# A third chunk of the contraction formed with Strassen's seven products in nine pairs of column blocks

## The chip, the cores and the metric

The kernel runs on one core of a Trainium2 chip. The metric is device time in microseconds (us) of one execution. TensorE multiplies, VectorE and ScalarE do elementwise work, GpSimd very little, and SyncE issues nearly all transfers.

## The reference

One layer of a hybrid encoder on x of shape (256, 2048) in float32. The part that matters here is a row of dense products, all with 2048 as the contracted length:

```python
h = rms_norm(x, norm_g)
proj = h @ w_in            # q, k, v, o, z, gates, xb, zb, ga, gb
ya = mlstm_branch(...)     # (256, 2048)
yb = rglru_branch(...)     # (256, 2048)
ya = ya @ w_branch_a
yb = yb @ w_branch_b
merged = sigmoid(ga) * ya + sigmoid(gb) * yb
y = rms_norm(x + merged @ w_out, final_g)
```

## The kernel before

**Precision.** TensorE multiplies in a reduced float32 format. Every operand is kept as a high part and a low part (x = hi + lo), and a product is the sum of three matmuls: hi by hi, hi by lo, lo by hi. So every weight tile that is loaded has to be split: ScalarE copies it into `whi` (line 124 or 160), VectorE subtracts it to make `wlo` (line 125 or 161).

**Tiling.** A weight matrix is cut into column blocks of 512 and into eight chunks of the contraction, each of 2 x 128 rows (`KC = 2`). One chunk of one block is a tile of 128 x 1024 (512 KB), loaded by SyncE into one of five `raw` buffers and split into one of four `whi` and one of four `wlo` buffers. The left operand has 256 rows, two blocks of 128. A chunk of one block takes 2 x 2 x 3 = 12 matmuls of 512 columns.

**The nine pairs.** In the last 40% of the kernel, column blocks are computed two at a time by `pair` (lines 144 to 231): two pairs each of w_branch_b (wb), the gb and the ga columns of w_in, and w_branch_a (wa), and one of w_out (wo). Between the wa pairs and the wo pair, one more block of wo is computed in plain form (`block_nat`). In a pair, the chunks listed in `S_WB`, `S_GB`, `S_GA`, `S_WA` and `S_WO` (lines 27 and 28) are not multiplied plainly. Such a chunk is seen as a 2 x 2 block matrix (two blocks of rows by two k halves, times two k halves by two column blocks), and Strassen's method in Winograd's form gives its four results with seven products instead of eight, each of three matmuls:

```python
t1[:, lf] = r1[:, rt_] - r1[:, lf]      # VectorE, 128x512 each
t1[:, rt_] = r2[:, lf] - r1[:, rt_]
t2[:, lf] = t1[:, rt_] + r1[:, lf]
t2[:, rt_] = r2[:, rt_] - t2[:, lf]
mm(p1, *xb(0, 0), b[:, lf], b[:, rt_], last)
mm(p5, *sf(0), h1[:, lf], l1[:, lf], last)
mm(p7, *sf(2), h1[:, rt_], l1[:, rt_], last)
mm(p6, *sf(1), h2[:, lf], l2[:, lf], last)
```

The remaining three products are added straight to the accumulators of the plain chunks. `b` is a split of half a tile (128 x 512, hi and lo side by side), and h1, h2, h3 with l1, l2, l3 are three `whi` and `wlo` tiles made from t1, t2 and the second loaded tile r2. The products p1, p5, p6 and p7 are gathered over the product chunks in four banks of the accumulator memory and combined once after the last of them by one ScalarE copy and four VectorE additions (lines 220 to 224). The chunks up to the last product chunk are run for both blocks in turn, the ones after it for one block and then for the other; at the end of each block comes an addition of the accumulator (line 230) and an epilogue. The plain chunks of a pair go through `load_chunk`.

**Forms.** The left operands of four of the seven products are sums of blocks of the left matrix. `make_form` (lines 233 to 247) makes them once for each chunk and each left matrix (yb, h, ya and m): an addition of hi and lo (line 239; not for yb), four 128 x 128 operations (lines 242 to 245), a ScalarE cast (246) and a VectorE low part (247). The result lies in one of four slots of the slot `PT` (for m in `E`). Its scratch has the tag `vhi`, of which there is one buffer; t1 of every product chunk has the same tag, and t2 has `vlo`. The forms of h are used by the gb and the ga pairs.

**Order.** The program is written in order, and a planner sets the final order on each engine from priorities and from its own model of time. The loads, splits and combinations stand in `urgent()` blocks, the forms don't.

Of the kernel before, what the change touches and what calls it, by code (L numbers as in the profile page):

```python
# [23 lines left out]
EPS = 1e-6  # L24
NEG = -1e30

S_WB, S_GB, S_GA, S_WA = [((0, 4), (0, 4))] * 4
S_WO = (0, 4)

PK_NORM, PK_HEAD, PK_CB, PK_CW, PK_BRG, PK_LAM = 0, 1, 2, 3, 7, 11  # L30
BLK_Q, BLK_K, BLK_V, BLK_O, BLK_Z, BLK_XB, BLK_ZB, BLK_GA, BLK_GB = 0, 2, 4, 8, 12, 16, 20, 24, 28
# [7 lines left out]
def hybrid_encoder(ctx: ExitStack, tc: tile.TileContext, x, xt, pk, bif, fg, wg, wi, wr, wa, wb, wo, out):  # L39
# [19 lines left out]
    def sl(tag, dt=F32, cols=4096):  # L59
        return slot.tile([P, cols], dt, tag=tag, name=name("s" + tag))  # L60
# [172 lines left out]
    def make_form(fm, full=None, parts=None):  # L233
        u = hp.tile([P, 2 * NB], F32, tag="vhi", name=name("sf"))
        if full is None:
            full = u[:, NB:]
            hi, lo = parts
            v = full if len(hi.shape) == 2 else full.rearrange("p (k s) -> p k s", s=S)
            dve.tensor_add(v, f(hi), f(lo))
        a11, a21, a12, a22 = [full[:, i * P:(i + 1) * P] for i in range(4)]  # L240
        s1, s2, s3, s4 = [u[:, i * P:(i + 1) * P] for i in range(4)]
        dve.tensor_add(s1, a21, a22)
        dve.tensor_sub(s2, s1, a11)
        dve.tensor_sub(s3, a11, a21)
        dve.tensor_sub(s4, a12, s2)
        act.copy(fm[:, :NB], u[:, :NB])
        dve.tensor_sub(fm[:, NB:], u[:, :NB], f(fm[:, :NB]))
# [674 lines left out]
    et_ = sl("E", F32R)  # L922
    mf_ = {kq: et_[:, i * 1024:(i + 1) * 1024] for i, kq in enumerate(S_WO)}
    for kq in S_WO:
        make_form(mf_[kq], parts=[t(kq * NB, (kq + 1) * NB) for t in (mh, ml)])
# [5 lines left out]

    pair((wo[0], wo[1]), mh, ml, mf_, S_WO, dst, b11, epi_wo)

# [91 lines left out]
```

## Time and profile before

| | |
|---|---|
| runs (three), median | 1030.87 us (1030.67 to 1031.13) |
| profiled execution | 1030.37 us, span from first to last instruction 1028.6 us |
| TensorE matmuls | 1019.5 us busy, 5124 of them |
| VectorE | 786.2 us busy, 1039 instructions |
| ScalarE | 580.1 us busy, 763 instructions |
| transfers | 199.32 MB, mean 194 GB/s |

Busy time is a union over an engine's instructions, so that overlapping ones are counted once. Matmuls are pipelined: the recorded length of one overlaps the next, and what one costs is read from the distance between starts. The stretch from 594 to 998.5 us holds the nine pairs.

### The profile page before, as it was taken

To read this page: it belongs to the slowest core of one execution; us is meant where nothing else is said; L and a number is where in the kernel's file an instruction comes from. 1 tells how busy PE (TensorE), PEld (TensorE's weight loads), DVE (VectorE), ACT (ScalarE), POOL (GpSimd) and SP (SyncE) were. 2 spreads that over 40 slices of the span, in tenths; PEclk is the share of its full clock that TensorE was granted. 3 is DMA by queue.
4 is the path that set the end of the run, shared out by engine and by line. 5 is a ranking of instruction groups with operands and counts; after the bars stand their busy time and mean duration, and the time that the engine had idled before them with its cause. 6 is when DMAs were issued, how large, how long until landed. Compare 5 with 4: busy or idle time off the path is not lost.

```text
span 1028.6 us, 13664 instructions
## 1 busy us (share of the span) xinstructions
PE 1019.5 (99%) x5124; PEld 867.3 (84%) x5124; DVE 786.2 (76%) x1039; ACT 580.1 (56%) x763; POOL 11.3 (1%) x35
## 2 busy tenths in 40 slices
PE   9999999999999999999999999999999999999997
PEld 9988888888888888888888888888888888888886
DVE  6787797596578649854977778887787877979784
ACT  7545457745765585559455555545554555454562
POOL 1000000000000000000000000000000000000000
PEclk9999999999999999999999999999999999999999
DMA  9654445554555555554655455555566645666562
GB/s 349 255 188 140 164 162 177 175 203 167 182 201 187 183 179 180 191 190 156 212 184 187 163 203 197 211 209 183 194 204 208 214 167 206 212 244 255 183 205 82
DMA packets 55954, 199.32 MB, mean 194 GB/s; under 512 B 6352, under 2 KB 6864, under 8 KB 55504
## 3 DMA queue, kind: packets, MB, share of 16 engines
q1 hardware_dynamic: 55024, 197.13, 55.1%
q10 hardware_dynamic: 864, 1.32, 0.4%
q8 instruction: 40, 0.66, 0.3%
q14 instruction: 26, 0.21, 0.1%
HBM read 196.33 MB, written 2.10 MB: 193 GB/s over the span
## 4 chain that ended last, share of the span: by engine, by line
PE 98%; DMA 1%; DVE 0%; SPq 0%; ACT 0%; issue 0%; DVEq 0%
PE acc L275 16%; PE acc L157 11%; PE acc L154 11%; PE acc L156 11%; PE acc L139 9%; PE acc L140 9%; PE acc L141 9%; PE acc L278 8%; PE aux L154 2%; PE aux L157 2%; PE aux L156 2%; PE aux L761 1%; PE aux L675 1%; PE aux L674 1%; PE aux L673 1%; PE aux L951 1%
## 5 line engine op out<-in xcount | busy, mean ns | idle before, releaser
L125 DVE TENSOR_TENSOR wlo<-raw,whi 128x1024 fp32r<-128x1024 f32 (+1 forms) x321 | 389.3, 1219 | 154.6 <-ACT whi L124 152.6
L124 ACT CAST whi<-raw 128x1024 fp32r<-128x1024 f32 (+1 forms) x321 | 334.4, 1048 | 267.7 <-PE acc L141 80.9
L275 PE MATMUL acc<-sHL,whi 128*128 128x512 f32 x704 | 178.6, 394 | 0.0
L139 PE MATMUL acc<-whi,sHL 128*128 128x512 f32 x416 | 162.4, 390 | 0.0
L140 PE MATMUL acc<-wlo,sHL 128*128 128x512 f32 x416 | 162.2, 390 | 0.0
L141 PE MATMUL acc<-whi,sHL 128*128 128x512 f32 x416 | 162.0, 389 | 0.0
L275 PEld LDWEIGHTS acc<-sHL,whi 128*128 128x128 f32 x704 | 127.0, 189 | 23.7
L278 PEld LDWEIGHTS acc<-sHL,wlo 128*128 128x128 f32 x704 | 96.1, 190 | 7.2
L156 PE MATMUL acc<-wlo,sHL 128*128 128x512 f32 x260 | 101.1, 389 | 0.0
L157 PE MATMUL acc<-whi,sHL 128*128 128x512 f32 x260 | 101.1, 389 | 0.0
L154 PE MATMUL acc<-whi,sHL 128*128 128x512 f32 x260 | 99.5, 389 | 0.0
L278 PE MATMUL acc<-sHL,wlo 128*128 128x256 f32 x704 | 99.2, 283 | 0.0
L141 PEld LDWEIGHTS acc<-whi,sHL 128*128 128x128 f32 x416 | 78.1, 188 | 16.3
L139 PEld LDWEIGHTS acc<-whi,sHL 128*128 128x128 f32 x416 | 78.2, 188 | 15.6
L140 PEld LDWEIGHTS acc<-wlo,sHL 128*128 128x128 f32 x416 | 78.2, 188 | 15.3
L160 ACT CAST whi<-t 128x1024 fp32r<-128x1024 f32 x36 | 37.9, 1053 | 57.4 <-PE acc L157 41.2
L157 PEld LDWEIGHTS acc<-whi,sHL 128*128 128x128 f32 x260 | 48.8, 188 | 10.2
L156 PEld LDWEIGHTS acc<-wlo,sHL 128*128 128x128 f32 x260 | 48.8, 188 | 10.2
L154 PEld LDWEIGHTS acc<-whi,sHL 128*128 128x128 f32 x260 | 48.8, 188 | 10.1
L161 DVE TENSOR_TENSOR wlo<-t,whi 128x1024 fp32r<-128x1024 f32 x36 | 44.0, 1223 | 14.6 <-ACT whi L160 14.6
L156 PE MATMUL acc<-wlo,sA 128*128 128x512 f32 x104 | 40.6, 390 | 0.0
L157 PE MATMUL acc<-whi,sB 128*128 128x512 f32 x104 | 40.5, 390 | 0.0
(314 smaller groups left out, 1435.2 us busy)
## 6 DMA issues: line engine op xcount, KB each, us to landing
raw<-wi SPq DMA_DIRECT2D x255, 512.0 KB, 3.6
raw<-wb SPq DMA_DIRECT2D x32, 512.0 KB, 3.7
raw<-wa SPq DMA_DIRECT2D x32, 512.0 KB, 3.7
raw<-wo SPq DMA_DIRECT2D x32, 512.0 KB, 4.4
raw<-wr SPq DMA_DIRECT2D x8, 512.0 KB, 3.6
sB<-x SPq DMA_DIRECT2D x4, 512.0 KB, 8.3
sA<-x SPq DMA_DIRECT2D x1, 2048.0 KB, 7.4
sA<-xt SPq DMA_DIRECT2D x7, 256.0 KB, 7.2
```

What stands on the lines that cost most here:

```text
L124: last_copy[0] = act.copy(hi[:, r], raw[:, r]).ins
L125: last_sub[0] = dve.tensor_sub(lo[:, r], raw[:, r], f(hi[:, r])).ins
L139: pe.matmul(ps[tb], a, wh, start=(k == 0), stop=False)
L140: pe.matmul(ps[tb], a, wl, start=False, stop=False)
L141: pe.matmul(ps[tb], b, wh, start=False, stop=(k == KT - 1))
L154: pe.matmul(ps, a, wh, start=id(ps) not in began, stop=False)
L156: pe.matmul(ps, a, wl, start=False, stop=False)
L157: pe.matmul(ps, b, wh, start=False, stop=stop)
L160: act.copy(hi, v)
L161: dve.tensor_sub(lo, v, f(hi))
L275: pe.matmul(ps[m], hi[:, o:o + P], hl_t[:, 2 * k * S:2 * (k + 1) * S], start=(k == 0), stop=False, skip_group_check=True)
L278: pe.matmul(ps[m][:, :S], lo[:, o:o + P], hhi(k * S, (k + 1) * S), start=False, stop=(k == KT - 1), skip_group_check=True)
```

## The change

The product form is used for the chunks 0, 2 and 4 of each pair in place of 0 and 4. Chunk 2 was a plain chunk for both blocks. For each of the nine pairs that means seven products where there were eight, one more b, t1, t2 and three more splits of 128 x 1024 in place of two; and one more form for each of yb, h, ya and m. The last product chunk is still 4, so that the combination stays where it was. The host lays out the weights of chunk 2 as those of 0 and 4. The slots that forms are put in follow from the order in the lists: for yb 0, 1 and 2 in place of 0 and 1; for h slot 3, and then 0 and 1 in place of 0; for ya slot 2, and then 0 and 1 in place of 0.

```diff
-S_WB, S_GB, S_GA, S_WA = [((0, 4), (0, 4))] * 4
-S_WO = (0, 4)
+S_WB, S_GB, S_GA, S_WA = [((0, 2, 4), (0, 2, 4))] * 4
+S_WO = (0, 2, 4)
```

## Rows read from the trace of the kernel before

**Rows 1.** The page: busy time, the chain that ended last, a group of casts.
```profile
PE 1019.5 (99%) x5124; PEld 867.3 (84%) x5124; DVE 786.2 (76%) x1039; ACT 580.1 (56%) x763; POOL 11.3 (1%) x35
...
PE 98%; DMA 1%; DVE 0%; SPq 0%; ACT 0%; issue 0%; DVEq 0%
...
L160 ACT CAST whi<-t 128x1024 fp32r<-128x1024 f32 x36 | 37.9, 1053 | 57.4 <-PE acc L157 41.2
```

**Rows 2.** Windows (busy by engine, clock, DMA): wb pair 2, gb pair 1, wo, all.
```profile
636.50:678.50 42.00, 42.00 (x187) 34.79 (x186) 36.41 (x46) 21.46 (x23) 0.00 (x0) 1.00 0.58 201
678.50:720.50 42.00, 42.00 (x188) 34.75 (x186) 33.44 (x35) 21.57 (x22) 0.00 (x0) 1.00 0.57 200
...
931.50:956.00 24.50, 24.50 (x118) 20.36 (x117) 21.95 (x28) 12.29 (x16) 0.00 (x0) 1.00 0.67 257
...
sum 404.50, PE 404.50 PEld 334.99 DVE 335.38 ACT 213.45 POOL 0.00; mean PE 40.45 PEld 33.50 DVE 33.54 ACT 21.35 POOL 0.00
```

**Rows 3.** Timeline of TensorE (start, length): first and last of 30 matmuls.
```profile
695.79 0.39 PE L154 MATMUL acc<-whi,sHL 128*128 128x512 f32 x1
...
702.37 0.39 PE L157 MATMUL acc<-whi,sHL 128*128 128x512 f32 x1
```

**Rows 4.** Timeline of VectorE, gb pair 2, from pair end to pair end.
```profile
720.70 1.22 DVE L230 TENSOR_TENSOR sD<-sD,acc 128x1024 f32<-128x1024 f32 x1 [0.37 <-PE acc L157]
...
729.48 1.22 DVE L125 TENSOR_TENSOR wlo<-raw,whi 128x1024 fp32r<-128x1024 f32 x1
730.61 0.69 DVE L161 TENSOR_TENSOR b<-raw,b 128x512 fp32r<-128x512 f32 x1
731.21 0.69 DVE L176 TENSOR_TENSOR t<-raw,raw 128x512 f32<-128x512 f32 x1
731.93 0.69 DVE L180 TENSOR_TENSOR t<-t,raw 128x512 f32<-128x512 f32 x1
...
762.86 1.22 DVE L230 TENSOR_TENSOR sD<-sD,acc 128x1024 f32<-128x1024 f32 x1 [0.36 <-PE acc L157]
```

**Rows 5.** Waits of VectorE and of ScalarE, 594 to 1000 us (total, times, longest).
```profile
DVE wlo L161 <- ACT whi L160: 31.4, 30, 1.5
...
ACT whi L124 <- PE acc L157: 62.0, 64, 1.7
ACT whi L160 <- PE acc L157: 61.6, 41, 1.9
...
ACT whi L160 <- DVE t L181: 8.3, 4, 3.1
```

**Rows 6.** Timeline ahead of gb: two forms, t1, low part, TensorE's first use.
```profile
652.60 0.69 DVE L239 TENSOR_TENSOR sf<-sHL 128x512 f32<-128x512 f32 x1
653.32 0.29 DVE L242 TENSOR_TENSOR sf<-sf 128x128 f32<-128x128 f32 x1
...
656.78 0.68 DVE L247 TENSOR_TENSOR sPT<-sf,sPT 128x512 fp32r<-128x512 f32 x1
...
666.23 0.69 DVE L247 TENSOR_TENSOR sPT<-sf,sPT 128x512 fp32r<-128x512 f32 x1
...
668.57 0.69 DVE L175 TENSOR_TENSOR t<-raw 128x512 f32<-128x512 f32 x1
...
672.64 1.22 DVE L161 TENSOR_TENSOR wlo<-t,whi 128x1024 fp32r<-128x1024 f32 x1
...
679.02 0.39 PE L156 MATMUL aux<-wlo,sPT 128*128 128x512 f32 x1
```

**Rows 7.** Timeline ahead of wo: second form, low part, TensorE's first use.
```profile
941.88 0.68 DVE L239 TENSOR_TENSOR sf<-sHL 128x512 f32<-128x512 f32 x1
...
946.60 0.68 DVE L247 TENSOR_TENSOR sE<-sf,sE 128x512 fp32r<-128x512 f32 x1
...
951.00 1.22 DVE L161 TENSOR_TENSOR wlo<-t,whi 128x1024 fp32r<-128x1024 f32 x1
...
957.53 0.39 PE L156 MATMUL aux<-wlo,sE 128*128 128x512 f32 x1
```

## The prediction

> **What bounds the kernel now.** I read the page first: TensorE's matmuls are busy 1019.5 us of a 1028.6 us span, and the chain of work that ended last is 98% TensorE [rows 1]. Next I cut the time in which the nine pairs run (594 to 998.5 us) into ten windows, one for each pair and one for the plain block ahead of the last pair [rows 2]. TensorE is busy in all 404.50 us of them at a granted clock of 1.00, which is the 2.4 GHz level; VectorE is busy 335.38 us (83%), ScalarE 213.45 us (53%), and the DMA engines about 0.6 of the time. So a matmul left out here shortens the kernel by one step of the matmul stream, as long as the weight tiles keep coming. The timeline of TensorE gives that step [rows 3]: 29 matmuls of 512 columns lie between the starts 695.79 and 702.37 us, so 6.58 / 29 = 0.2269 us each (a matmul's recorded 0.39 us overlaps the next). Two ends of a pair, 720.70 and 762.86 us [rows 4], are 42.16 us apart for 186 matmuls: the same 0.2267 us.
>
> The reader should then look at VectorE, since it is the engine that the change loads. In the list of waits [rows 5], ScalarE's copies of weight tiles waited 62.0 us (plain tiles) and 61.6 us (product tiles) for TensorE to finish with an old tile, and only 8.3 us for VectorE. That is back-pressure: four buffers each of whi and wlo are full and the preparation is ahead. VectorE's own wait for the copies of product tiles, 31.4 us, is mostly the same back-pressure handed on.
>
> **What the change does, part by part.**
>
> *Matmuls.* A chunk of a pair takes 2 x 2 x 2 x 3 = 24 matmuls in plain form and 7 x 3 = 21 in product form. Nine pairs give 27 matmuls fewer, each with its weight load, which runs beside the matmuls: 27 x 0.2267 = 6.12 us. All of it lies on the path that sets the end.
>
> *VectorE, chunks.* Two plain subtractions go and eight operations come: one 512-wide for b, four 512-wide for t1 and t2, three 1024-wide for the low parts. By recorded length [rows 4] that is 5 x 0.69 + 3 x 1.22 = 7.1 against 2 x 1.22 = 2.4. But consecutive operations overlap: in the same rows a 1024-wide one that starts at 729.48 is followed at 730.61 (step 1.13 us), and 512-wide ones step by 0.60 (730.61 to 731.21) or, where one reads what the last wrote, 0.72 (731.21 to 731.93). By steps it is about 3.1 + 3.4 = 6.5 against 2.27, so 4.2 us more for each of nine chunks, 37.8 us.
>
> *VectorE, forms.* Four forms are added. One for the wb pairs lies before 594 us, where this window's sum doesn't count it. The ones of h, ya and m lie inside: the add steps 0.72 (652.60 to 653.32 [rows 6]), four 128-wide operations of 0.29 us recorded step about 0.2 each, the low part 0.60, together 1.95 us; three make 5.9 us.
>
> *The balance.* VectorE goes from 335.4 to 335.4 + 37.8 + 5.9 = 379.1 us, and the time it has shrinks from 404.5 to 398.4: 95%, with 19.3 us left. By pair: the first gb pair goes to 33.44 + 4.2 = 37.6 of 41.3 us, which is easy; the second wb pair to 36.41 + 4.2 + 1.95 = 42.6 of 41.3, over by 1.3 us, which the first gb pair can take; the plain wo block to 21.95 + 1.95 = 23.9 of 24.5 [rows 2]. Within a pair the new order is product, plain, product, plain, product: one product and one plain chunk cost VectorE 6.5 + 2.3 = 8.8 us while TensorE takes (21 + 24) x 0.2267 = 10.2 us, so the lead holds. A plain tile feeds 12 matmuls (2.7 us), and a copy and a subtraction after a buffer comes free take about 2.4 us, so the buffers carry a local shortage of two to five us.
>
> The Trainium skill, page "VectorE: DVE Perf Modes", section "The DRAIN you can't avoid", says that a next operation does not start until the pipe has emptied, and so speaks against the change. Here the rows show the next one starting 0.09 us before the recorded end of the one in front (730.61 against 729.48 + 1.22 = 730.70). By the rule the time would be that of rival D below, by the rows it is the sum above.
>
> *ScalarE.* Four casts replace two: three of 1.05 us [rows 1] and one half as wide (0.6 us by that) instead of two of 1.05 us, 1.7 us for a chunk, 15 us in all, and four small casts. 213 becomes about 231 of 398 us; other work doesn't queue up behind it.
>
> *DMA.* A product chunk loads the same two 512 KB pieces as two plain chunks do, on the same queue in the same order: nothing, and the cover is not thin, as the share is about 0.6. The extra instructions are small.
>
> *The one order that tightens.* t1 and every form use one buffer (tag vhi). So all forms made between two pairs must end before the next pair's t1 may start, and behind that t1 stand the cast of h1, the low part and TensorE's first product. Before gb this chain holds two forms: the first runs from 652.60 to the end of its low part at 657.46, the second from there to 666.92, t1 starts at 668.57, the low part of h1 runs from 672.64 to 673.86, and TensorE wants it at 679.02 [rows 6]: 5.2 us of margin. A third form costs between 1.95 us (nothing but its work) and 9.5 us (what the second took, with recombination and plain tiles in between); nearest is the first one's 4.9 us, which fits. The extreme would stall TensorE by 9.5 - 5.2 = 4.3 us. Before wo the chain holds two forms and gets a third: the second takes 941.88 to 947.2, the low part of h1 starts at 951.00 and ends at 952.2, and TensorE wants it at 957.53 [rows 7], so 5.3 us of margin against 1.95 to 5.4 us. Before wa a second form is added too, but by the code the old one is written into a slot that the last product chunk still reads and has to wait for it, so the new one, whose slot is read by the middle chunk, fits into that wait. I take 0.5 us of stall in all; the bounds are 0 and about 5.
>
> *Sum.* The profiled execution took 1030.37 us, 1.77 more than its span; the runs' median is 1030.87. 1030.37 - 6.12 + 0.5 = 1024.75 for that execution, so 1025.25 against the median: 1025.2.
>
> **The rivals.**
> A, the forecast: TensorE stays fed but for small gaps, 1024.3 to 1026.3. For it: TensorE without a gap, and the copies' 123 us of waits for full buffers. Chance 0.60.
>
> B: VectorE sets the pace at a few places, above all at the entries of gb and wo and where two wa pairs meet (there each block has two more 1024-wide operations). It loses 1.5 to 5 us of the 6.1: 1026.4 to 1029.9. For it: the second wb pair's sum over 41.3 us. Against: free VectorE time in the next pair. Chance 0.20.
>
> C, the other side: product chunks bring handshake waits that don't go away. A product tile waits in turn for VectorE's t, ScalarE's cast, VectorE's low part; VectorE waited 31.4 us before such low parts in 18 chunks, 1.74 us each. If those stayed and nine chunks added theirs, the stage would take 379.1 + 27 x 1.74 = 426 us, 21.6 us longer: about 1052. It decides from the point where more than 404.5 - 379.1 = 25.4 us of VectorE's waits can't be filled; just beyond it the time is 1033 to 1036. Against: ScalarE's own waits say that these are full buffers, 61.6 us for TensorE against 8.3 us for t. Chance 0.11, mostly near the point.
>
> D: VectorE is held for each operation's recorded length. 1.22 us in place of a step of 1.13 is 8% more, so the 379.1 us become 409.4, which is 4.9 us longer than the stage is now: 1035.8. The steps in [rows 4] are against it. Chance 0.03. This is the time by the rule of the Trainium skill named above.
>
> E: the change does not do what it says, because the order of instructions, which a planner sets from its own times, places forms or product tiles late in each pair: 0.7 us lost in each of nine pairs eats 6.1 us, so 1030 to 1031. For it: that order is made anew for the changed program. Against: in the present one no gap came of it in ten windows. Chance 0.06.
>
> **How the numbers follow.** A change of 0.2% (2.06 us) is about what a measurement of this kernel can tell. Faster means under 1028.8: A and three quarters of B, 0.75. Slower means over 1032.9: C and D less 0.02 for C just at its point, 0.12. Same is the rest of B (0.05), E (0.06) and that 0.02 of C, 0.13. The range that holds 8 in 10 takes A and B with their bounds: 1024.0 to 1029.8.
>
> **What will show it.** Right: 5097 matmuls instead of 5124; 81 product-tile low parts on VectorE instead of 54; TensorE without gaps at a step of 0.2267 us and a pair 41.5 us long; VectorE busy about 379 us of the stage; ScalarE still waiting mostly for TensorE before its copies. Rival B shows as TensorE waiting for wlo at the start of gb or of wo; C as VectorE waiting over 1 us for product casts while ScalarE waits for t; D as 1.22 us steps; E as a gap in every pair. The prediction is wrong if TensorE's busy time falls by 6 us and its idle time grows by as much.

## The result and the profile after

The changed kernel takes 1034.58 us (median of six runs, 1032.82 to 1036.94) against 1030.77 us for the kernel before on the same chip: a ratio of 1.004, 95% interval 1.0027 to 1.0053. It is slower by 0.4%, where 1025.2 us was forecast. The profiled execution is the lowest of its six runs, 1032.82 us with a span of 1031.1 us.

The page of the kernel after, its busy time, the chain that ended last and the group of casts, against [rows 1]:

```profile
PE 1016.8 (99%) x5097; PEld 861.0 (84%) x5097; DVE 825.2 (80%) x1116; ACT 594.2 (58%) x785; POOL 11.4 (1%) x35
...
PE 90%; DVE 5%; DMA 3%; issue 1%; ACT 0%; SPq 0%; DVEq 0%
...
L160 ACT CAST whi<-t 128x1024 fp32r<-128x1024 f32 x54 | 56.7, 1051 | 54.2 <-DVE t L181 21.0
```

The 27 matmuls are gone (5124 to 5097), but the chain is 90% TensorE where it was 98%: VectorE and transfers now stand in it. Before, the casts of t waited mostly for TensorE to give back a buffer; now they wait mostly for VectorE's t.

Windows of the kernel after (columns as in [rows 2]). The sum is that of 594 to 1001 us, in which its nine pairs lie:

```profile
636.00:678.00 42.00, 42.00 (x185) 34.46 (x184) 37.49 (x53) 20.79 (x23) 0.00 (x0) 1.00 0.55 188
678.00:720.00 42.00, 38.96 (x166) 30.46 (x165) 37.50 (x43) 22.89 (x24) 0.00 (x0) 1.00 0.61 202
720.00:762.00 42.00, 42.00 (x187) 34.79 (x186) 38.46 (x44) 23.72 (x25) 0.00 (x0) 1.00 0.61 200
...
sum 407.00, PE 402.32 PEld 329.51 DVE 372.78 ACT 227.30 POOL 0.00; mean PE 201.16 PEld 164.75 DVE 186.39 ACT 113.65 POOL 0.00
```

The reader is to see that one window of a pair is short of matmuls, 166 in place of 187, and that the next is full. The loss is not spread over the pairs; it sits where gb begins, and at wo. To size it I went through the starts of all matmuls from 585 us on and added up by how much each step was over its own length (0.227 us for 512 columns, 0.120 for 256, 0.066 for 128; excesses under 0.05 us left out): 0.62 us before, 8.24 us after, of which 4.4 us lie between 678 and 696 us (entry of gb) and 3.0 us between 960 and 974 us (entry of wo). Below, this sum is called the gaps. The page's busy time is no measure of it: it fell by 2.7 us only (1019.5 to 1016.8), because a matmul's recorded 0.39 us reaches 0.16 us past its step and so covers part of each gap. TensorE at the entry of gb, kernel after (the brackets show idle time and who ended it):

```profile
678.70 0.39 PE L157 MATMUL aux<-b,sHL 128*128 128x512 f32 x1
679.81 0.73 PE L154 MATMUL aux<-whi,sPT 128*128 128x512 f32 x2 [0.71 <-ACT whi L160]
681.54 0.50 PE L154 MATMUL aux<-whi,sPT 128*128 128x512 f32 x1 [1.00 <-ACT whi L160]
...
683.50 0.50 PE L156 MATMUL aux<-wlo,sPT 128*128 128x512 f32 x1
...
685.87 0.73 PE L154 MATMUL aux<-whi,sPT 128*128 128x512 f32 x2 [0.94 <-ACT whi L160]
```

From 678.70 to 679.81 is a step of 1.11 us where 0.227 is due. Most of what TensorE waits for at gb is ScalarE's casts of t1 and t2, which wait in turn for VectorE. What VectorE did ahead of it (it answers to [rows 6]), and a pair further on (to [rows 4]):

```profile
663.20 1.22 DVE L125 TENSOR_TENSOR wlo<-raw,whi 128x1024 fp32r<-128x1024 f32 x1
664.34 0.68 DVE L222 TENSOR_TENSOR sE<-aux,sE 128x512 f32<-128x512 f32 x1
...
666.07 0.68 DVE L247 TENSOR_TENSOR sPT<-sf,sPT 128x512 fp32r<-128x512 f32 x1
666.67 0.68 DVE L223 TENSOR_TENSOR sE<-aux,sE 128x512 f32<-128x512 f32 x1
667.27 0.68 DVE L224 TENSOR_TENSOR sE<-aux,sE 128x512 f32<-128x512 f32 x1
...
669.00 0.68 DVE L161 TENSOR_TENSOR b<-raw,b 128x512 fp32r<-128x512 f32 x1
669.61 0.68 DVE L239 TENSOR_TENSOR sf<-sA,sB 128x512 f32<-128x512 f32 x1
...
674.17 0.69 DVE L247 TENSOR_TENSOR sPT<-sf,sPT 128x512 fp32r<-128x512 f32 x1 [0.69 <-ACT sPT L246]
676.70 0.69 DVE L161 TENSOR_TENSOR b<-raw,b 128x512 fp32r<-128x512 f32 x1 [1.83 <-ACT b L160]
677.31 0.68 DVE L175 TENSOR_TENSOR t<-raw 128x512 f32<-128x512 f32 x1
...
679.96 1.22 DVE L161 TENSOR_TENSOR wlo<-t,whi 128x1024 fp32r<-128x1024 f32 x1
...
717.58 1.22 DVE L230 TENSOR_TENSOR sD<-sD,acc 128x1024 f32<-128x1024 f32 x1
...
759.01 1.21 DVE L230 TENSOR_TENSOR sD<-sD,acc 128x1024 f32<-128x1024 f32 x1
```

Chunk 0's b is split at 669.00 (667.97 before). Then the third form (669.61 to 674.86, from sA and sB, so that of ya) holds the one vhi buffer that t1 needs. When it is done, t1 still doesn't start: in VectorE's order the b of product chunk 2 now stands ahead of it, and that b waits 1.83 us for ScalarE. Why, ScalarE's timeline of the kernel after shows:

```profile
673.52 0.62 ACT L246 CAST sPT<-sf 128x512 fp32r<-128x512 f32 x1 [4.38 <-DVE sf L245]
676.05 0.62 ACT L160 CAST b<-raw 128x512 fp32r<-128x512 f32 x1 [1.91 <-DMA raw<-wi]
678.71 1.05 ACT L160 CAST whi<-t 128x1024 fp32r<-128x1024 f32 x1 [2.04 <-DVE t L176]
```

ScalarE waited for a transfer, that of chunk 2's first tile. So chunk 0's t1, whose own tile had long landed, waited for the data of a later chunk. It starts at 677.31 (before: 668.57), and the low part of h1 at 679.96 (before: 672.64): 7.3 us later, where the margin was 5.2.

It doesn't end there. t1 and t2 read the loaded tiles, and these hold `raw` buffers. SyncE's loads in the kernel after:

```profile
671.45 0.33 SPq L170 DMA_DIRECT2D raw<-wi  x1
679.35 0.33 SPq L171 DMA_DIRECT2D raw<-wi  x1
```

Chunk 2's second tile (line 171) is issued only at 679.35, after chunk 0's t2 began at 678.63. So the delay reaches chunk 2 too.

VectorE at the entry of wo, kernel after ([rows 7]):

```profile
951.70 0.69 DVE L247 TENSOR_TENSOR sE<-sf,sE 128x512 fp32r<-128x512 f32 x1 [0.69 <-ACT sE L246]
952.90 0.69 DVE L161 TENSOR_TENSOR b<-raw,b 128x512 fp32r<-128x512 f32 x1 [0.51 <-ACT b L160]
953.51 0.68 DVE L175 TENSOR_TENSOR t<-raw 128x512 f32<-128x512 f32 x1
...
956.17 1.22 DVE L161 TENSOR_TENSOR wlo<-t,whi 128x1024 fp32r<-128x1024 f32 x1
```

The same picture: third form, then a later chunk's b, then t1; the low part is 5.2 us later than in [rows 7], which is its whole margin of 5.3. It still ends in time, at 957.39, where TensorE first uses it at 958.94. The gaps come behind it:

```profile
960.84 1.22 DVE L161 TENSOR_TENSOR wlo<-raw,whi 128x1024 fp32r<-128x1024 f32 x1
```
```profile
962.11 0.50 PE L156 MATMUL acc<-wlo,sHL 128*128 128x512 f32 x1 [0.74 <-DVE wlo L161]
```
```profile
969.85 0.62 ACT L160 CAST b<-raw 128x512 fp32r<-128x512 f32 x1 [7.41 <-DMA raw<-wo]
```

TensorE waits first for the low part of chunk 0's second loaded tile (960.84 to 962.06), which in VectorE's order stands behind chunk 2's t1 (959.63). SyncE could issue chunk 2's second tile only at 955.55, when chunk 0's t2 had read its first tile, and at 969.85 ScalarE has stood 7.41 us for a load before the b of chunk 4; the next gaps, 969.74 to 974, lie there.

Waits of the kernel after, 594 to 1000 us, against [rows 5]:

```profile
ACT whi L124 <- PE acc L157: 33.7, 31, 1.9
ACT whi L160 <- PE acc L157: 20.8, 17, 4.7
ACT whi L160 <- DVE t L181: 20.6, 12, 3.2
ACT b L160 <- DMA raw<-wi: 19.6, 12, 2.5
ACT whi L160 <- DVE t L176: 14.0, 8, 2.3
...
DVE wlo L161 <- ACT whi L160: 4.6, 5, 1.2
```

The waits for full buffers fell from 62.0 and 61.6 us to 33.7 and 20.8. They were the measure of the lead, and more than half of it is gone. Most of that fall is no sign of the gaps, though: in run 1 below, which has hardly any, these two waits are 45.6 and 19.8 us.

### The profile page after: what moved, and what is told of

Read it like the earlier page. It is cut to its first block, busy times and chain, and to the rows that moved or that the text cites. A ratio compares the mean times of both kernels' runs of the same rounds, so it can differ in the third digit from the quotient of the medians.

```text
span 1031.1 us, 13715 instructions
## 1 busy us (share of the span) xinstructions
PE 1016.8 (99%) x5097; PEld 861.0 (84%) x5097; DVE 825.2 (80%) x1116; ACT 594.2 (58%) x785; POOL 11.4 (1%) x35
## 4 chain that ended last, share of the span: by engine, by line
PE 90%; DVE 5%; DMA 3%; issue 1%; ACT 0%; SPq 0%; DVEq 0%
PE acc L275 16%; PE acc L139 8%; PE acc L140 8%; PE acc L141 8%; PE acc L156 8%; PE acc L157 8%; PE acc L154 8%; PE acc L278 8%; PE aux L156 2%; PE aux L157 2%; PE aux L154 2%; DMA raw<-wo 2%; DVE wlo L125 2%; DMA raw<-wi 2%; PE aux L761 1%
## 5 line engine op out<-in xcount | busy, mean ns | idle before, releaser
L125 DVE TENSOR_TENSOR wlo<-raw,whi 128x1024 fp32r<-128x1024 f32 (+1 forms) x303 | 365.5, 1216 | 142.3 <-ACT whi L124 140.7
L124 ACT CAST whi<-raw 128x1024 fp32r<-128x1024 f32 (+1 forms) x303 | 314.7, 1048 | 239.4 <-PE acc L141 78.2
L139 PE MATMUL acc<-whi,sHL 128*128 128x512 f32 x416 | 162.4, 390 | 0.0
L140 PE MATMUL acc<-wlo,sHL 128*128 128x512 f32 x416 | 162.2, 390 | 0.0
L141 PE MATMUL acc<-whi,sHL 128*128 128x512 f32 x416 | 162.0, 389 | 0.0
L141 PEld LDWEIGHTS acc<-whi,sHL 128*128 128x128 f32 x416 | 78.1, 188 | 16.3
L139 PEld LDWEIGHTS acc<-whi,sHL 128*128 128x128 f32 x416 | 78.2, 188 | 15.6
L140 PEld LDWEIGHTS acc<-wlo,sHL 128*128 128x128 f32 x416 | 78.2, 188 | 15.4
L156 PE MATMUL acc<-wlo,sHL 128*128 128x512 f32 x230 | 89.6, 390 | 0.7 <-DVE wlo L161 0.7
L157 PE MATMUL acc<-whi,sHL 128*128 128x512 f32 x230 | 89.5, 389 | 0.0
L160 ACT CAST whi<-t 128x1024 fp32r<-128x1024 f32 x54 | 56.7, 1051 | 54.2 <-DVE t L181 21.0
L154 PE MATMUL acc<-whi,sHL 128*128 128x512 f32 x230 | 87.6, 389 | 0.0
L161 DVE TENSOR_TENSOR wlo<-t,whi 128x1024 fp32r<-128x1024 f32 x54 | 65.3, 1218 | 3.9 <-ACT whi L160 3.5
L156 PEld LDWEIGHTS acc<-wlo,sHL 128*128 128x128 f32 x230 | 43.2, 188 | 10.4 <-DVE wlo L161 1.2
L154 PEld LDWEIGHTS acc<-whi,sHL 128*128 128x128 f32 x230 | 43.2, 188 | 9.0
L157 PEld LDWEIGHTS acc<-whi,sHL 128*128 128x128 f32 x230 | 43.2, 188 | 8.8
L160 ACT CAST b<-raw 128x512 fp32r<-128x512 f32 x27 | 16.8, 621 | 45.4 <-DMA raw<-wi 19.6
L156 PE MATMUL acc<-wlo,sA 128*128 128x512 f32 x92 | 36.1, 392 | 0.0
```

The source lines that it names most:

```text
L124: last_copy[0] = act.copy(hi[:, r], raw[:, r]).ins
L125: last_sub[0] = dve.tensor_sub(lo[:, r], raw[:, r], f(hi[:, r])).ins
L139: pe.matmul(ps[tb], a, wh, start=(k == 0), stop=False)
L140: pe.matmul(ps[tb], a, wl, start=False, stop=False)
L141: pe.matmul(ps[tb], b, wh, start=False, stop=(k == KT - 1))
L154: pe.matmul(ps, a, wh, start=id(ps) not in began, stop=False)
```

## The experiments

Three theories (1, 2 and 3 in the expectations). **Buffer**: the one buffer that forms and t1 share makes t1 late at gb and wo. **Load**: VectorE simply has too much to do. **Order**: what costs is the later chunk's b ahead of t1, which waits for a transfer. Times are medians; each ratio is to the kernel before in the same job (1030.62 to 1030.81 us), with its 95% interval.

**1. A scratch of its own for the forms.** The buffer `xp` of an earlier stage is free by then.

```diff
-        u = hp.tile([P, 2 * NB], F32, tag="vhi", name=name("sf"))
+        u = xp.rearrange("p a b -> p (a b)")[:, :2 * NB]
```

> The changed kernel, with the scratch of the forms moved out of the buffer that t1 uses (into the conv input's tile, which is dead by then). Theory 1, the shared buffer: t1 no longer waits for the chain of forms, the gaps of TensorE at the entries of gb (4.2 us) and wo (3.3 us) shrink to under 1.5 us together, and the time is 1024.7 to 1026.5 us. Theory 2, VectorE's load: the same work stands in the same places, the gaps stay, 1032 to 1035 us. Theory 3, the order and the loads: a VectorE or ScalarE queue that waits at the b of the next product chunk for its transfer keeps about half of the gaps, 1027 to 1031 us.

Measured: 1026.05 us (1025.67 to 1026.73), ratio 0.9956 [0.9943, 0.9968]; gaps 1.00 us. The same number of instructions on every engine, 8.5 us less than the kernel after. VectorE and SyncE in this kernel, ahead of gb:

```profile
668.67 0.68 DVE L175 TENSOR_TENSOR t<-raw 128x512 f32<-128x512 f32 x1
...
673.55 0.28 DVE L245 TENSOR_TENSOR xp<-xp 128x128 f32<-128x128 f32 x1
673.75 1.21 DVE L161 TENSOR_TENSOR wlo<-t,whi 128x1024 fp32r<-128x1024 f32 x1
```

```profile
671.93 0.33 SPq L170 DMA_DIRECT2D raw<-wi  x1
673.66 0.33 SPq L171 DMA_DIRECT2D raw<-wi  x1
```

t1 starts 8.6 us earlier, ahead of a form's last operations (line 245) instead of behind them; the low part starts at 673.75 and chunk 2's second tile is issued 5.7 us earlier. At wo, t1 starts at 941.00 where it was 953.51. Buffer is right; Load, as the whole cause, is out.

**2. The same scratch in the kernel before**, as a control.

> Control: the kernel before with the same move of the scratch. All theories: TensorE has no gap there that could go, 1030.8 us within 1 us.

Measured: 1030.59 us, ratio 0.9999 [0.999, 1.0008]. With two chunks the shared buffer cost nothing.

**3. Two product chunks in the wo pair alone.**

```diff
-S_WO = (0, 2, 4)
+S_WO = (0, 4)
```

> The changed kernel with the wo pair left at chunks 0 and 4. Theories 1, 2 and 3: the gap at wo (3.3 us) goes and the 0.68 us that its third chunk saved come back; about 2.6 us less than the changed kernel, 1031 to 1033 us; the gap at gb stays at 3 to 5 us.

Measured: 1030.65 us (1029.53 to 1032.52), ratio 1.0003 [0.9994, 1.0012]. That is a little under the expected 1031 to 1033. The gap at wo is gone and that at gb is still 4.1 us. It is 3.9 us under the kernel after, though three matmuls more (0.68 us) were put back; so wo costs about 4.6 us in the median.

**4. The kernel before with one more form ahead of gb and one ahead of wo**, which nothing reads.

```diff
         h_form(kq, i)
+    h_form(2, 1)
     ya_form(k_ya[0], 2)
...
         make_form(mf_[kq], parts=[t(kq * NB, (kq + 1) * NB) for t in (mh, ml)])
+        if kq == 0:
+            make_form(et_[:, 2048:3072], parts=[t(2 * NB, 3 * NB) for t in (mh, ml)])
```

> The kernel before (two product chunks) with one more form ahead of gb and one ahead of wo that nothing reads, so that the chain in the shared buffer is as long as in the changed kernel, without the third product chunk. Theory 1 in its strong form, the chain alone: gaps of 1 to 4 us at gb and up to 2 us at wo, 1032 to 1036 us. Theory 2 and 3: the lead is full before these places, the two forms cost VectorE 4 us that it has, 1030.5 to 1031.5 us.

Measured: 1031.27 us, ratio 1.0006 [0.9997, 1.0015]; gaps 0.86 us, 0.24 more than before. VectorE ahead of gb in this kernel:

```profile
673.80 0.69 DVE L247 TENSOR_TENSOR sPT<-sf,sPT 128x512 fp32r<-128x512 f32 x1 [0.69 <-ACT sPT L246]
674.53 0.69 DVE L175 TENSOR_TENSOR t<-raw 128x512 f32<-128x512 f32 x1
...
677.19 1.22 DVE L161 TENSOR_TENSOR wlo<-t,whi 128x1024 fp32r<-128x1024 f32 x1
```

A miss for the strong form of Buffer. The third form delays the low part by 4.6 us, to 677.19, and the margin of 5.2 swallows that, as the prediction had reckoned. The chain of forms is needed for the loss but is not enough; the third product chunk has to come to it.

**5. The order: a product chunk's b is put behind the t2 (VectorE) and the cast of h1 (ScalarE) of the chunk before**; the buffer stays shared.

```diff
...
+                with ExitStack() as es:
+                    for i in order_b:
+                        es.enter_context(tc.issue_after(i))
-                split(b[:, lf], b[:, rt_], r1[:, lf])
+                    split(b[:, lf], b[:, rt_], r1[:, lf])
...
-                split(h1, l1, t1)
+                act1 = act.copy(h1, t1).ins
+                dve.tensor_sub(l1, t1, f(h1))
...
-                dve.tensor_sub(t2[:, rt_], r2[:, rt_], t2[:, lf])
+                order_b[:] = [act1, dve.tensor_sub(t2[:, rt_], r2[:, rt_], t2[:, lf]).ins]
```

> The changed kernel with the shared buffer left as it is; only the issue order is held: the split of a product chunk's b comes behind t2 (VectorE) and the cast of h1 (ScalarE) of the product chunk before. Theory 1, the chain of forms in the shared buffer: t1 still starts when the third form ends, so the gaps stay, 1032 to 1035 us, at most 1 us less than the changed kernel. Theory 3, the order: VectorE's wait of 1.8 us ahead of t1 at gb and that of 0.5 us at wo go, 1.5 to 3 us less than the changed kernel, 1030 to 1032.5 us.

Measured: 1032.01 us (1029.28 to 1033.52), ratio 1.001 [1.0002, 1.0019]: 2.6 us under the kernel after. t1 at gb starts at 675.43, as soon as the form is done, and the low part at 678.10, 1.9 us earlier; yet the gaps at gb are still 3.5 us and at wo 2.6. VectorE in this kernel, whose line 184 makes the low part of h1:

```profile
678.10 1.22 DVE L184 TENSOR_TENSOR wlo<-t,whi 128x1024 fp32r<-128x1024 f32 x1
```

Order is a part, the smaller one. How large it is depends on the measure: the medians differ by 2.6 us, the gaps of the two profiled executions by 1.2 (7.04 against 8.24), and the one of the kernel after is its fastest.

**6. The form of ya made after the gb pairs**, so that two forms stand ahead of gb.

```diff
-    ya_form(k_ya[0], 2)
     for p in range(2):
...
     ga = []
+    ya_form(k_ya[0], 2)
     for p in range(2):
```

> The changed kernel with one form (ya, chunk 0) made after the gb pairs in place of ahead of them, in the same shared buffer: the chain ahead of gb has two forms, as in the kernel before, and the third product chunk stays. Theory 1: the gap at gb (4.2 us) shrinks to under 1 us, that at wo stays, about 3.5 us less than the changed kernel, 1029.5 to 1031.5 us. Theory 2, VectorE's load: one form's 2 us of work moved, the gap shrinks by 2 us at most, 1032 to 1033.5 us.

Measured: 1030.44 us (1027.87 to 1032.27), ratio 0.9995 [0.9986, 1.0003]: 4.1 us under the kernel after. t1 at gb starts at 669.04 and the gaps there are 0.7 us; wo, left alone, has 4.7 us in this trace. So gb's loss too needs the chain of forms; in the medians wo costs about 4.6 us (run 3) and gb 4.1.

**7. Scratch and order together**: the edits of runs 1 and 5.

> Own scratch for the forms and the order of e5 together. Theory 1: the gaps were already gone with the scratch alone (1026.05 us), the order brings nothing, 1025.5 to 1026.7 us. Theory 3: what is left over the 1024.6 us of 27 matmuls fewer is order, 1024.5 to 1025.5 us.

Measured: 1025.78 us (1025.4 to 1028.4), ratio 0.9957 [0.9945, 0.9969]. No different from run 1: with a scratch of its own, the order has nothing left to cost.

**8. Run 1 with the product chunks 0, 1 and 4.** The same work, but two product chunks stand next to each other.

```diff
-S_WB, S_GB, S_GA, S_WA = [((0, 2, 4), (0, 2, 4))] * 4
-S_WO = (0, 2, 4)
+S_WB, S_GB, S_GA, S_WA = [((0, 1, 4), (0, 1, 4))] * 4
+S_WO = (0, 1, 4)
```

> Own scratch, and the product chunks are 0, 1 and 4 in place of 0, 2 and 4: the same work, but two product chunks in a row at the start of each pair. Theory of the local balance (VectorE 6.5 us for a product chunk against 4.8 us of TensorE, made up for by plain chunks): behind a pair's end with its recombination and epilogue the lead is short, two in a row cost 13 us of VectorE in 9.5 us, 1 to 2 us of gap in most of nine pairs, 1032 to 1042 us. Theory of the sum alone (VectorE 95% full over the stage): the position doesn't matter, 1025.5 to 1027 us.

Measured: 1030.6 us (1028.5 to 1032.82), ratio 1.0 [0.9991, 1.0008]; gaps 4.65 us in its fastest run, at the entries of gb and wo and between the wa pairs, not in all nine pairs. The time lies between the two expectations. 4.5 us over run 1 at equal total work: how much product work comes in a row matters as well as how much there is.

**9. Run 1 with four product chunks in the wo pair.**

```diff
-S_WO = (0, 2, 4)
+S_WO = (0, 2, 4, 6)
```

> The kernel after with the scratch of its own (1026.05), and a fourth of four product chunks in the one pair over wo instead of three (three matmuls fewer there, VectorE with about one more set of forms, splits and T1 to T4). Theory that only the shared buffer cost time: three matmuls of 0.2267 us fewer and no gap at wo, so 1025.2 to 1025.6. Theory that the lead of VectorE is used up within a pair: a gap of 1 to 3 us at wo, so 1026.5 to 1029.

Measured: 1026.56 us (1025.68 to 1027.39), ratio 0.9961 [0.9948, 0.9973], with gaps of 1.5 us at 975 to 980 us in the profile. Three more matmuls are gone (0.68 us) and nothing is won. 0.5 us against run 1 is less than the intervals tell apart; the gaps say that the lead is used up within this pair.

**10, 11, 12. How much room VectorE has.** Run 10 is run 1 with T2's last subtraction issued twice in each product chunk; run 11 is run 1 with a subtraction whose result nothing reads, written behind the last low part; run 12 is the kernel before (with the scratch) with T2's last subtraction twice.

```diff
-                dve.tensor_sub(t2[:, rt_], r2[:, rt_], t2[:, lf])
+                for _ in range(2):
+                    dve.tensor_sub(t2[:, rt_], r2[:, rt_], t2[:, lf])
```
```diff
                 split(h3, l3, r2)
+                z = hp.tile([P, 2 * NB], F32, tag="zz", name=name("zz"))
+                dve.tensor_sub(z[:, lf], f(xhi(0, NB)), f(xlo(0, NB)))
```

> The kernel after with the scratch of its own (1026.05), in which the last subtraction of T2 is issued twice in every product chunk: 27 idle subtractions of 0.60 us, 16.2 us more of VectorE over 402 us, which takes it from 371.6 to about 388 (96.5%); the output is unchanged. Theory that VectorE's total is not the bound and the lead before each chunk covers 0.6 us: 1026 to 1027.5. Theory that VectorE's load sets the pace (rival B of the prediction): 1029 to 1035, with gaps on TensorE in most of the nine pairs.

> The kernel after with the scratch of its own (1026.05), with one more 128x512 subtraction behind the last low part of every product chunk, into a tile that nothing reads: 27 x 0.60 = 16.2 us more of VectorE, as in the run with the doubled subtraction (1041.5), but no product tile waits for its result and no loaded tile is held longer by it. Theory that VectorE's total is the bound once it passes about 92% of the stretch: about the same loss, 1036 to 1042. Theory that the longer path from the loaded tiles to the product tiles made that loss: 1026 to 1028.

> The kernel before with the scratch of its own (1030.59), with the last subtraction of T2 issued twice in its 18 product chunks: 10.8 us more of VectorE, which goes from 335 to 346 of 404.5 us (86%), and each product tile's path 0.60 us longer. Theory of VectorE's total: nothing, 1030.4 to 1031. Theory of the longer path: part of 18 x 0.60 us, 1033 to 1041.

Measured: run 10, 1041.5 us (1038.31 to 1042.79), ratio 1.011 [1.0094, 1.0125], gaps 12.8 us in its fastest run; run 11, 1033.03 us (1030.13 to 1034.29), ratio 1.002 [1.0009, 1.003], gaps 9.5 us in one of its slowest, 1034.18 us; run 12, 1030.48 us, ratio 0.9998 [0.999, 1.0007], gaps 0.54 us. The sums of the windows from 594 us to the end of the pairs, one line each of run 1, run 10, run 11 and run 12:

```profile
sum 399.50, PE 399.49 PEld 330.04 DVE 369.14 ACT 227.81 POOL 0.00; mean PE 199.75 PEld 165.02 DVE 184.57 ACT 113.90 POOL 0.00
```
```profile
sum 412.00, PE 405.99 PEld 327.54 DVE 383.98 ACT 222.86 POOL 0.00; mean PE 203.00 PEld 163.77 DVE 191.99 ACT 111.43 POOL 0.00
```
```profile
sum 408.00, PE 403.15 PEld 328.69 DVE 384.52 ACT 225.95 POOL 0.00; mean PE 201.58 PEld 164.35 DVE 192.26 ACT 112.97 POOL 0.00
```
```profile
sum 404.50, PE 404.50 PEld 335.02 DVE 342.42 ACT 213.07 POOL 0.00; mean PE 202.25 PEld 167.51 DVE 171.21 ACT 106.53 POOL 0.00
```

Run 10 lies 6.5 us beyond the upper end of its larger expectation, and run 11 between its two: 16.2 us more of VectorE costs 7.0 us where no data waits for it, and 15.5 us where the product tiles wait for it too. So VectorE's load counts once it is at 92% (369.14 of 399.50 us), and it counts more on the path of the tiles. The two runs don't part load and path cleanly: the planner put 14 of run 11's 27 subtractions directly ahead of an operation on t or of its low part, which then stands 0.60 us longer behind it. At 83% to 85% a longer path costs nothing (run 12). And VectorE never gets beyond 93% or 94% busy (383.98 / 412, 384.52 / 408) while TensorE starves: the rest is what it stands, in its own order, for casts and transfers, as the waits of run 11 from 594 to 1010 us show:

```profile
DVE wlo L125 <- ACT whi L124: 6.2, 6, 1.7
DVE t L175 <- DMA raw<-wi: 4.8, 4, 3.4
DVE wlo L161 <- ACT whi L160: 4.4, 6, 1.2
```

## Why the prediction was wrong

**The step that failed** is the term of 0.5 us of stall, with bounds of 0 and about 5, under "The one order that tightens". The place and the chain were named; the term measured 7.4 us in the trace: 4.4 at gb and 3.0 at wo. Run 1 shows that both need the shared buffer, and run 6 shows it once more for gb alone. The size was wrong for three reasons.

*The chain was priced as its forms alone.* The third form cost 4.6 us (run 4), close to the 4.9 taken, and alone fitted the margin. But t1 then stood behind a later chunk's b, which waited for a transfer: 2.5 us at gb (674.86 to 677.31). With that b held behind t2, the kernel is 2.6 us faster in the median (run 5). That b didn't exist in the kernel before, and the prediction didn't ask what the order would put between the last form and t1.

*The margin was read as if it were paid once.* 7.3 us late against a margin of 5.2 would be 2.1 us at gb, not 4.4; 5.2 against 5.3 would be nothing at wo, not 3.0. A late t1 holds `raw` buffers, so the next product chunk's tile is issued late (679.35 against 673.66 in run 1), and the tiles behind the first are late too. That the buffers carry the delay is read from the trace; no run had more of them. The prediction put the DMA at nothing because queue and sizes were unchanged; what changed was when the buffers came free.

*The 19.3 us that VectorE had left were not to be had.* The balance gave 95% and called it enough. VectorE's busy time came out near the forecast, 372.78 us against 379.1, but runs 10 and 11 show that at this load further work costs 43% to 96% of its length (7.0 and 15.5 of 16.2 us). So a lead once lost at gb isn't won back soon: in run 5 the low part of h1 ends at 679.32, only 0.3 us behind the 679.02 of [rows 6], and 3.5 us are lost over the chunks that follow, where run 4, ending at 678.41 and with two product chunks a pair, loses almost nothing. That this difference is the thinner lead is an inference from these two runs and runs 10 to 12; no run varied it by itself.

**The sum.** 1030.37 - 6.12 + 7.4 = 1031.65 us; the profiled execution took 1032.82. Of the other 1.17 us, 0.54 is a later start of the first pair (594.30 for 593.76 us), which the prediction's sum left out, and 0.2 lies in smaller gaps; some 0.4 us stay unassigned. In the balance, a form's steps of 0.72, four times 0.2 and 0.60 add up to 2.1 us, not 1.95; half a microsecond in 379, which changes nothing. The median is another 1.8 us up, and no trace shows those runs.

**Right:** 27 matmuls fewer; the step of 0.227 us; a pair free of gaps is 41.43 us long (717.58 to 759.01; 41.5 forecast); 81 product low parts (54 from t and 27 from raw); ScalarE 227.3 us (231 forecast). With the scratch apart, run 1 gains 4.6 of the 6.12 us in its median and comes near the forecast's 1025.2; of the missing 1.5 us, 0.4 are gaps and 0.9 a later start of the first pair (594.66 us). **Not right:** that ScalarE's copies would still wait mostly for TensorE; from 594 to 1000 us they wait 54.5 us for it, but also 34.6 us for t and, before b, 45.3 us for loads (19.6 in the kernel before).

**The rivals.** B was right in mechanism and in two of its places (gb and wo), and its price of 1.5 to 5 us was too small: it holds for one entry, and both struck. Its sign, TensorE waiting for wlo, came at wo; at gb TensorE waited mostly for whi. Its "against", free VectorE time in the next pair, was the same mistake as the balance. B should have ended on the other side of the kernel before. C predicted a wait at every product tile: VectorE's wait before product low parts fell from 31.4 to 4.6 us, so it is out. E predicted a gap in each pair: there are two, but the planner's order does have a share (run 5). D's time, 1035.8 us, is close to the result by chance: in the rows above a 1024-wide operation is followed after 1.14 us (663.20, 664.34) and a 512-wide one after 0.60 (666.67, 667.27), as before. The rule that the prediction took from the Trainium skill, "VectorE: DVE Perf Modes", section "The DRAIN you can't avoid", is not what these rows show; but the same section goes on that a next operation that isn't held starts earlier, and with that the rows agree.

The Trainium skill, page "Perfetto Trace Analysis", section "Identifying Performance Opportunities", says that the same gap repeating on the engine that should be saturated can mean that there is too little memory for the next tile, the number of buffers for one. Run 1 agrees as to the cause: a buffer of their own for the forms takes the gaps from 8.24 to 1.00 us. But they didn't repeat from pair to pair; they came at two of the places where forms are made.

## What to carry to other kernels

When a change adds a producer to a buffer with a single slot, list all who take that slot in order, and ask what the new order puts between them and the engine that starves: the waits add up, and each also holds the buffers of the loads behind it. An engine that works in order and waits on two others isn't free to the last per cent: in these runs added work on VectorE cost nothing at 85% and up to nearly its full length from 92% on. Before calling a change that saves matmuls a loss, try it with a buffer apart: here that one line makes 1034.6 us into 1026.05, faster than both kernels.

## What was not expected

Kernels whose TensorE has gaps also seem to vary more from run to run. The kernel before spans 1.1 us (six runs), run 1 1.1 us (five) and run 12 0.7 us (eleven); the kernel after spans 4.1 us (six), runs 5, 6, 8 and 11 between 4.2 and 4.4 us, and run 10 4.5 us. Single runs stand out without many gaps too: one of run 7's five took 1028.4 us where the others lie within 0.6 us, and one of 29 of the kernel before 1032.72 us. The late tiles wait for transfers, and a transfer's time that varies would then reach the end; that is argued, not shown. It also means that one profile of such a kernel is one of several outcomes: the kernel after's is its fastest run, so the 7.4 us of stalls are more likely too small than too large.
